# The last 256 rows of a row mean: blocks split over partitions, two-source sums and an indicator matmul

## The chip, the cores and the metric

The kernel runs on one core of one Trainium2 chip. The metric is the device time in microseconds (us) of one execution; lower is better.

## The reference

```python
x = np.random.randn(64, 256, 8192).astype(np.float32)   # 16384 rows of 8192, 537 MB
return np.mean(x, axis=2)                               # 16384 means
```

## The kernel before

63 "pairs" of 256 rows (two rows a partition, 8 MiB, called pair 1 to 63 below) stream through three buffers, and VectorE (called DVE in the profiles) reduces each with one instruction. The last 256 rows are two blocks of 128 rows: the first comes as one load, the last in four column chunks (9/16, 1/4, 1/8 and 1/16 of the row). DVE and ScalarE (ACT) share the sums of the last pair and of these blocks. Declarations and most waits are cut. (In the profiles SPq is the queue on which SyncE issues transfers, PE is TensorE and POOL is GpSimd.)

```python
# SyncE: all loads
for t in range(NP):                                   # NP = 63, NBUF = 3
    if t >= NBUF:
        eng.wait_ge(dve_sem, t - NBUF + 1)            # buffer free again
    eng.dma_start(bufs[t % NBUF][:], x_pair[t]).then_inc(in_sems[t % NBUF], 16)
...
for c in range(NCH):                                  # last 128 rows: 4 column chunks
    sl = slice(offs[c], offs[c] + CH[c])
    eng.dma_start(buf2[:, sl], x_one[T2][:, sl]).then_inc(ch_sems[c], 16)
...
eng.wait_ge(fin_sem, 3)                               # the last store
eng.dma_start(out_q[4 * T2 : 4 * T2 + 4, :], fint[0:P:32, :]).then_inc(out_sems[2], 16)

# VectorE
eng.tensor_reduce(dst, bufs[k][:].rearrange("p (r l) -> p r l", r=R), X, ADD)   # every pair
...
eng.tensor_reduce(part[:, 2:3], buf2[:, offs[3] : offs[3] + CH[3]], X, ADD)     # last chunk
...
eng.tensor_reduce(fin[:, 0:1], part[:, 0:6], X, ADD).then_inc(fin_sem, 1)       # join 6 parts
eng.transpose(fint[:], fin[:]).then_inc(fin_sem, 1)                             # 32x32 blocks
eng.tensor_scalar(fint[:], fint[:], inv, None, mybir.AluOpType.mult).then_inc(fin_sem, 1)

# ScalarE: its share, for example
eng.activation(src, src, Copy, accum_out=dst).then_inc(act_sem, 1)
```

The 32x32 transpose leaves the last 128 results in partitions 0, 32, 64 and 96, 32 in each, so the last store reads four partitions.

## Time and profile before

| what | value | where it is read |
|---|---|---|
| time | 1246.21 us (1245.99 to 1246.72, 3 runs) | timed runs |
| span of the profiled run | 1244.7 us | page |
| one pair to the next, landing to landing | 19.355 us (mean) | landings in the trace |
| landing of pair 63, then the last landing | 1222.02, 1241.64 us | landings in the trace |
| last landing to the issue of the last store | 1.39 us | landing and timeline |
| that issue to the end | 1.69 us | timeline and span |

First the page of the kernel before: busy tenths of DVE and of the DMA engines in 40 equal slices, GB/s in each slice, and the chain of waits.

```profile
DVE  2898988989889889898898988989889898898897
...
DMA  9999999999999999999999999999999999999998
GB/s 436 415 430 438 438 438 438 430 413 438 438 438 438 438 436 411 434 438 438 438 438 438 425 417 438 438 438 438 438 432 411 438 438 438 438 438 436 417 428 373
...
DMA 70%; DVE 29%; issue 0%; SPq 0%; DVEq 0%
...
buf<-in_x_dram SPq DMA_DIRECT2D x63, 40.7
...
buf<-in_x_dram SPq DMA_DIRECT2D x1, 256.0 KB, 20.4
```

The DMA engines are full in all slices but the last: the page gives the packets of the loads' queue 99.8% of the 16 engines' span. A pair is 8,388,608 bytes and one lands every 19.355 us on average, which is 433.4 GB/s. The last number of an issue line is the median time from issue to landing: 40.7 us for a pair, about two periods, so a load always has others queued before it. The chain gives DVE 29% because a load is issued when DVE frees a buffer.

Next the timeline of the end of the kernel before (start, duration, engine, line, operation, operands, and in brackets the idle time and what ended it).

```profile
1202.70 17.22 DVE L121 TENSOR_REDUCE res<-buf 128x2 f32<-128x16384 f32 x1 [2.13 <-DMA buf<-in_x_dram]
...
1222.05 8.69 DVE L133 TENSOR_REDUCE res<-buf 128x1 f32<-128x8192 f32 x1 [2.13 <-DMA buf<-in_x_dram]
...
1231.76 4.42 DVE L135 TENSOR_REDUCE res<-buf 128x1 f32<-128x4096 f32 x1 [1.03 <-DMA buf<-in_x_dram]
...
1237.27 2.42 DVE L137 TENSOR_REDUCE part<-buf 128x1 f32<-128x2176 f32 x1 [1.09 <-DMA buf<-in_x_dram]
...
1241.04 1.06 ACT L159 ACTIVATE buf<-buf 128x1024 f32<-128x1024 f32 x1
1241.66 0.69 DVE L143 TENSOR_REDUCE part<-buf 128x1 f32<-128x512 f32 x1 [0.69 <-DMA buf<-in_x_dram]
...
1242.38 0.16 DVE L149 TENSOR_REDUCE fin<-part 128x1 f32<-128x6 f32 x1
1242.58 0.21 DVE L151 STREAM_TRANSPOSE fint<-fin 128x32 f32<-128x32 f32 x1
1242.82 0.18 DVE L153 TENSOR_SCALAR fint<-fint 128x32 f32<-128x32 f32 x1
1243.03 0.61 SPq L110 DMA_DIRECT2D out_dram<-fint  x1
```

DVE waits for a transfer before each piece. After the last landing come a 0.69 us reduction, the joining of the six parts (three short DVE instructions), and the store. Only the time after 1241.64 us is not covered by the loads: 3.1 us, 0.25% of the span.

### The profile page before, as it was taken

The numbers are of one execution on the slowest core, as the hardware profiler recorded it, in microseconds if no ns is written. First come the engines' busy times: TensorE is split into PE (matmuls) and PEld (weight loads), VectorE is DVE, ScalarE is ACT, GpSimd is POOL, SyncE is SP. The second block draws the span as 40 slices with busy tenths as digits, with TensorE's granted clock in tenths as the row PEclk, the third lists the DMA queues.
The fourth block names the chain that finished last, engine by engine and source line by source line (L and its number), as shares of the span: only waits on it lengthen the run. The fifth ranks groups of instructions, "written<-read, shape, count | busy, mean of one in ns | idle before, by whom it ended". The sixth has DMA issues, their size and how long they took to land.

```text
span 1244.7 us, 315 instructions
## 1 busy us (share of the span) xinstructions
PE 1.7 (0%) x6; PEld 0.6 (0%) x6; DVE 1085.6 (87%) x70; ACT 17.2 (1%) x14; POOL 0.8 (0%) x7
## 2 busy tenths in 40 slices
PE   0000000000000000000000000000000000000000
PEld 0000000000000000000000000000000000000000
DVE  2898988989889889898898988989889898898897
ACT  0000000000000000000000000000000000000005
POOL 0000000000000000000000000000000000000000
DMA  9999999999999999999999999999999999999998
GB/s 436 415 430 438 438 438 438 430 413 438 438 438 438 438 436 411 434 438 438 438 438 438 425 417 438 438 438 438 438 432 411 438 438 438 438 438 436 417 428 373
DMA packets 9874, 536.94 MB, mean 431 GB/s; under 512 B 1106, under 2 KB 1170, under 8 KB 1426
## 3 DMA queue, kind: packets, MB, share of 16 engines
q1 hardware_dynamic: 9874, 536.94, 99.8%
HBM read 536.87 MB, written 0.07 MB: 431 GB/s over the span
## 4 chain that ended last, share of the span: by engine, by line
DMA 70%; DVE 29%; issue 0%; SPq 0%; DVEq 0%
DMA buf<-in_x_dram 70%; DVE res L121 29%; DVEq L121 0%; SPq L101 0%; DVE part L143 0%; SPq L95 0%; DVE fint L151 0%; DVE fint L153 0%; DVE fin L149 0%
## 5 line engine op out<-in xcount | busy, mean ns | idle before, releaser
L121 DVE TENSOR_REDUCE res<-buf 128x16384 f32 (+1 forms) x62 | 1067.6, 17220 | 152.3 <-DMA buf<-in_x_dram 152.3
L159 ACT ACTIVATE buf<-buf 128x1024 f32<-128x1024 f32 (+3 forms) x5 | 15.0, 2994 | 1221.7 <-DMA buf<-in_x_dram 1221.6
L133 DVE TENSOR_REDUCE res<-buf 128x1 f32<-128x8192 f32 x1 | 8.7, 8685 | 2.1 <-DMA buf<-in_x_dram 2.1
L135 DVE TENSOR_REDUCE res<-buf 128x1 f32<-128x4096 f32 x1 | 4.4, 4419 | 1.0 <-DMA buf<-in_x_dram 1.0
L137 DVE TENSOR_REDUCE part<-buf 128x1 f32<-128x2176 f32 x1 | 2.4, 2421 | 1.1 <-DMA buf<-in_x_dram 1.1
L184 PE MATMUL ps<-ident,res 128*63 128x128 f32 x2 | 0.7, 434 | 1230.8 <-DVE res L133 1230.8
L159 ACT ACT_TABLE_LOAD x1 | 1.3, 1283 | 1.8 <-PEq L220 1.8
L143 DVE TENSOR_REDUCE part<-buf 128x1 f32<-128x512 f32 x1 | 0.7, 686 | 0.7 <-DMA buf<-in_x_dram 0.7
L139 DVE TENSOR_REDUCE part<-buf 128x1 f32<-128x1024 f32 x1 | 1.2, 1220 | 0.1
L159 ACT ACTIVATION_READ_ACCUMULATOR buf<-buf 128x1 f32 x5 | 0.9, 186 | 0.0
L184 PEld LDWEIGHTS ps<-ident,res 128*63 128x63 f32 x2 | 0.3, 202 | 1230.8 <-issue 1230.8
L188 PE MATMUL psone<-ident,res 128*1 128x128 f32 x2 | 0.6, 421 | 0.0
L187 PE MATMUL psone<-ident,res 128*1 128x128 f32 x2 | 0.6, 397 | 4.7 <-DVE res L135 4.7
L169 ACT ACTIVATE outsb<-ps 63x128 f32<-63x128 f32 x2 | 0.4, 264 | 0.0
L79 POOL TENSOR_SCALAR_AFFINE_SELECT ident<-ident 128x128 f32<-128x128 f32 x1 | 0.3, 292 | 0.2 <-POOL ident L77 0.2
L171 ACT ACTIVATE out1sb<-psone 1x128 f32<-1x128 f32 x1 | 0.3, 266 | 1.5 <-PE psone L188 1.5
L188 PEld LDWEIGHTS psone<-ident,res 128*1 128x1 f32 x2 | 0.3, 128 | 0.2
L151 DVE STREAM_TRANSPOSE fint<-fin 128x32 f32<-128x32 f32 x1 | 0.2, 212 | 0.0
L153 DVE TENSOR_SCALAR fint<-fint 128x32 f32<-128x32 f32 x1 | 0.2, 181 | 0.0
L77 POOL MEMSET ident<- 128x128 f32 x1 | 0.2, 204 | 0.0
L149 DVE TENSOR_REDUCE fin<-part 128x1 f32<-128x6 f32 x1 | 0.2, 159 | 0.0
L76 POOL MEMSET fin<- 128x32 f32 x1 | 0.1, 125 | 1.3 <-POOLq L220 1.3
(5 smaller groups left out, 0.5 us busy)
## 6 DMA issues: line engine op xcount, KB each, us to landing
buf<-in_x_dram SPq DMA_DIRECT2D x1, 4096.0 KB, 31.1
buf<-in_x_dram SPq DMA_DIRECT2D x1, 2304.0 KB, 17.3
buf<-in_x_dram SPq DMA_DIRECT2D x1, 1024.0 KB, 19.4
buf<-in_x_dram SPq DMA_DIRECT2D x63, 40.7
buf<-in_x_dram SPq DMA_DIRECT2D x1, 512.0 KB, 20.2
buf<-in_x_dram SPq DMA_DIRECT2D x1, 256.0 KB, 20.4
out_dram<-outsb SPq DMA_DIRECT2D x1, 63.0 KB
out_dram<-out1sb SPq DMA_DIRECT2D x1, 0.5 KB
```

Of the source, the lines that this page charges most:

```text
L79: eng.affine_select(out=ident[:], in_=ident[:], compare_op=mybir.AluOpType.not_equal, fill=1.0, base=0, pattern=[[-1, P]], channel_multipl ...
L121: eng.tensor_reduce(dst, bufs[k][:].rearrange("p (r l) -> p r l", r=R), X, ADD).then_inc(dve_sem, 1)
L133: eng.tensor_reduce(res[:, t, 0:1], bufs[t % NBUF][:, :L], X, ADD).then_inc(dve_sem, 1)
L135: eng.tensor_reduce(res1[:, 0:1], buf1[:, : L // 2], X, ADD).then_inc(dve_sem, 1)
L137: eng.tensor_reduce(part[:, 0:1], buf2[:, :s0], X, ADD).then_inc(dve_sem, 1)
L139: eng.tensor_reduce(part[:, 1:2], buf2[:, offs[1] : offs[1] + s1], X, ADD).then_inc(dve_sem, 1)
L143: eng.tensor_reduce(part[:, 2:3], buf2[:, offs[3] : offs[3] + CH[3]], X, ADD).then_inc(dve_sem, 1)
L159: eng.activation(src, src, Copy, accum_out=dst).then_inc(act_sem, 1)
L169: eng.activation(outsb[:, :, r], ps[r][:], Copy, scale=inv).then_inc(cp_sem, 1)
L184: eng.transpose(ps[r][:], res[:, :, r], ident[:]).then_inc(pe_sem, 1)
L187: eng.matmul(psone[:], res1[:, 0:1], ident[:], start=True, stop=False)
L188: eng.matmul(psone[:], res1[:, 1:2], ident[:], start=False, stop=True).then_inc(pe_sem, 1)
```

## The change

The change puts the last 256 rows into blocks of 128, 64, 32 and 32 rows. A block of n rows is spread over all 128 partitions, 128/n parts a row. Each piece is summed by one DVE instruction that adds its two halves element by element and accumulates; ACT no longer sums. TensorE multiplies each column of partial sums with an indicator matrix, which adds up the parts of a row and leaves a block's results as one row in PSUM (the tiles `psb`). The 256 results gather in one row of one partition and go out in one store. The diff, cut to its core:

```diff
-    CH = [9 * L // 16, L // 4, L // 8, L // 16]
+    BLOCKS = [(128, [L]), (64, [L // 2]), (32, [L // 4])]
+    BLOCKS.append((32, [L // 8, 5 * L // 64, 3 * L // 64]))
...
+            src = x_rows[row : row + n].rearrange("r (q l) -> (r q) l", q=P // n)
...
+            eng.tensor_tensor(ind64[:], ident[:, 0:P:2], ident[:, 1:P:2], ADD)   # GpSimd
+            eng.tensor_tensor(ind32[:], ind64[:, 0:64:2], ind64[:, 1:64:2], ADD)
...
-            eng.dma_start(out_q[4 * T2 : 4 * T2 + 4, :], fint[0:P:32, :])
+            eng.dma_start(out_pair[NP : NP + 1, :], lastsb[:])
...
+            def fast(dst, run, scale=1.0):
+                h = run.shape[-1] // 2
+                return eng.tensor_tensor_reduce(
+                    out=run[:, 0:h], in0=run[:, 0:h], in1=run[:, h:],
+                    scale=scale, scalar=0.0, op0=ADD, op1=ADD, accum_out=dst,
+                )
...
+            for i, (k, n, src, place) in enumerate(pieces):
+                eng.wait_ge(ch_sems[i], 16)
+                fast(part[:, i : i + 1], place, inv).then_inc(part_sem, 1)
+            eng.wait_ge(pe_sem, R + NBLK)
+            eng.tensor_copy(lastsb[:, EARLY:], psb[-1][:, :n]).then_inc(last_sem, 1)
...
-            acc(part[:, 5:6], buf2[:, offs[2] : offs[2] + CH[2]])               # ACT's sums
...
+                mm = eng.matmul(
+                    psb[k][:, :n], part[:, i : i + 1], ind[n][:], start=start, stop=stop
+                )
```

The two sums of the last pair use the same `fast`; the other 62 pairs keep their reduction.

More of the change, by code (lines that the diff above doesn't have):

```diff
@@ L27, in bass_global_avg_pool_1d_kernel @@
     NBUF = 3
-    CH = [9 * L // 16, L // 4, L // 8, L // 16]
-    assert sum(CH) == L
-    NCH = len(CH)
+    BLOCKS = [(128, [L]), (64, [L // 2]), (32, [L // 4])]
+    BLOCKS.append((32, [L // 8, 5 * L // 64, 3 * L // 64]))
+    assert sum(n for n, _ in BLOCKS) == R * P
+    assert all(sum(ch) * P == n * L for n, ch in BLOCKS)
+    NBLK = len(BLOCKS)
+    EARLY = sum(n for n, _ in BLOCKS[:-1])
+    NCH = sum(len(ch) for _, ch in BLOCKS)
     x_rows = x.rearrange("b c l -> (b c) l")
     x_pair = x_rows.rearrange("(t p r) l -> t p (r l)", p=P, r=R)
-    x_one = x_rows.rearrange("(t p) l -> t p l", p=P)
-    out_flat = out.rearrange("b c -> (b c)")
-    out_pair = out_flat.rearrange("(t n) -> t n", n=R * P)
-    out_one = out_flat.rearrange("(t p) -> t p", p=P)
-    out_q = out_flat.rearrange("(t q) -> t q", q=32)
-    T1 = R * NP
-    T2 = R * NP + 1
+    out_pair = out.rearrange("b c -> (b c)").rearrange("(t n) -> t n", n=R * P)
     with ExitStack() as ctx:
@@ L45, in bass_global_avg_pool_1d_kernel @@
         res = E(nc.sbuf_tensor("res", [P, NP, R], f32))
-        res1 = E(nc.sbuf_tensor("res1", [P, 2], f32))
-        part = E(nc.sbuf_tensor("part", [P, 8], f32))
-        fin = E(nc.sbuf_tensor("fin", [P, 32], f32))
-        fint = E(nc.sbuf_tensor("fint", [P, 32], f32))
+        part = E(nc.sbuf_tensor("part", [P, NCH], f32))
         ident = E(nc.sbuf_tensor("ident", [P, P], f32))
+        ind64 = E(nc.sbuf_tensor("ind64", [P, 64], f32))
+        ind32 = E(nc.sbuf_tensor("ind32", [P, 32], f32))
+        ind = {128: ident, 64: ind64, 32: ind32}
         outsb = E(nc.sbuf_tensor("outsb", [NP, P, R], f32))
-        out1sb = E(nc.sbuf_tensor("out1sb", [1, P], f32))
+        lastsb = E(nc.sbuf_tensor("lastsb", [1, R * P], f32))
         ps = [E(nc.psum_tensor(f"ps{r}", [NP, P], f32)) for r in range(R)]
-        psone = E(nc.psum_tensor("psone", [1, P], f32))
+        psb = [E(nc.psum_tensor(f"psb{k}", [1, P], f32)) for k in range(NBLK)]
         in_sems = [E(nc.semaphore(f"in_sem{i}")) for i in range(NBUF)]
-        one_sem = E(nc.semaphore("one_sem"))
         ch_sems = [E(nc.semaphore(f"ch_sem{i}")) for i in range(NCH)]
         dve_sem = E(nc.semaphore("dve_sem"))
-        act_sem = E(nc.semaphore("act_sem"))
+        part_sem = E(nc.semaphore("part_sem"))
         prep_sem = E(nc.semaphore("prep_sem"))
@@ L63, in bass_global_avg_pool_1d_kernel @@
         cp_sem = E(nc.semaphore("cp_sem"))
-        fin_sem = E(nc.semaphore("fin_sem"))
-        out_sems = [E(nc.semaphore(f"out_sem{i}")) for i in range(3)]
-        b1 = NP % NBUF
-        b2 = (NP + 1) % NBUF
-        buf1 = bufs[b1]
-        buf2 = bufs[b2]
-        offs = [sum(CH[:i]) for i in range(NCH)]
-        s0 = CH[0] // 2 - L // 64
-        s1 = CH[1] // 2
+        last_sem = E(nc.semaphore("last_sem"))
+        out_sems = [E(nc.semaphore(f"out_sem{i}")) for i in range(2)]
+        pieces = []
+        row, at = NP * R * P, 0
+        for k, (n, ch) in enumerate(BLOCKS):
+            src = x_rows[row : row + n].rearrange("r (q l) -> (r q) l", q=P // n)
+            col = 0
+            for w in ch:
+                place = bufs[(NP + min(k, 1)) % NBUF][:, at + col : at + col + w]
+                pieces.append((k, n, src[:, col : col + w], place))
+                col += w
+            row += n
+            at = at + col if k else 0
         def gpsimd_program(eng):
-            eng.memset(fin[:], 0.0).then_inc(prep_sem, 1)
             eng.memset(ident[:], 0.0).then_inc(prep_sem, 1)
-            eng.wait_ge(prep_sem, 2)
+            eng.wait_ge(prep_sem, 1)
             eng.affine_select(
@@ L87, in gpsimd_program @@
             ).then_inc(prep_sem, 1)
+            eng.wait_ge(prep_sem, 2)
+            eng.tensor_tensor(ind64[:], ident[:, 0:P:2], ident[:, 1:P:2], ADD).then_inc(
+                prep_sem, 1
+            )
+            eng.wait_ge(prep_sem, 3)
+            eng.tensor_tensor(ind32[:], ind64[:, 0:64:2], ind64[:, 1:64:2], ADD).then_inc(
+                prep_sem, 1
+            )
         first = len(nc.main_func.blocks[0].instructions)
@@ L95, in sync_program @@
                 eng.dma_start(bufs[t % NBUF][:], x_pair[t]).then_inc(in_sems[t % NBUF], 16)
-            eng.wait_ge(dve_sem, NP - NBUF + 1)
-            eng.dma_start(buf1[:, :L], x_one[T1]).then_inc(one_sem, 16)
-            eng.wait_ge(dve_sem, NP - NBUF + 2)
-            for c in range(NCH):
-                sl = slice(offs[c], offs[c] + CH[c])
-                eng.dma_start(buf2[:, sl], x_one[T2][:, sl]).then_inc(ch_sems[c], 16)
+            for i, (k, n, src, place) in enumerate(pieces):
+                if i < 2:
+                    eng.wait_ge(dve_sem, NP - NBUF + 1 + i)
+                eng.dma_start(place, src).then_inc(ch_sems[i], 16)
             eng.wait_ge(cp_sem, 2)
@@ L106, in sync_program @@
             )
-            eng.wait_ge(cp_sem, 3)
-            eng.dma_start(out_one[T1 : T1 + 1, :], out1sb[:]).then_inc(out_sems[1], 16)
-            eng.wait_ge(fin_sem, 3)
-            eng.dma_start(out_q[4 * T2 : 4 * T2 + 4, :], fint[0:P:32, :]).then_inc(
-                out_sems[2], 16
-            )
+            eng.wait_ge(cp_sem, R + NBLK - 1)
+            eng.wait_ge(last_sem, 1)
+            eng.dma_start(out_pair[NP : NP + 1, :], lastsb[:]).then_inc(out_sems[1], 16)
             for s in out_sems:
@@ L123, in pair @@
                 ).then_inc(dve_sem, 1)
+            def fast(dst, run, scale=1.0):
+                h = run.shape[-1] // 2
+                return eng.tensor_tensor_reduce(
+                    out=run[:, 0:h],
+                    in0=run[:, 0:h],
+                    in1=run[:, h:],
+                    scale=scale,
+                    scalar=0.0,
+                    op0=ADD,
+                    op1=ADD,
+                    accum_out=dst,
+                )
             trips = (NP - 1) // NBUF
@@ L131, in vector_program @@
             t = NP - 1
-            eng.wait_ge(in_sems[t % NBUF], 16 * (t // NBUF + 1))
-            eng.tensor_reduce(res[:, t, 0:1], bufs[t % NBUF][:, :L], X, ADD).then_inc(dve_sem, 1)
-            eng.wait_ge(one_sem, 16)
-            eng.tensor_reduce(res1[:, 0:1], buf1[:, : L // 2], X, ADD).then_inc(dve_sem, 1)
-            eng.wait_ge(ch_sems[0], 16)
-            eng.tensor_reduce(part[:, 0:1], buf2[:, :s0], X, ADD).then_inc(dve_sem, 1)
-            eng.wait_ge(ch_sems[1], 16)
-            eng.tensor_reduce(
-                part[:, 1:2], buf2[:, offs[1] : offs[1] + s1], X, ADD
-            ).then_inc(dve_sem, 1)
-            eng.wait_ge(ch_sems[3], 16)
-            eng.tensor_reduce(
-                part[:, 2:3], buf2[:, offs[3] : offs[3] + CH[3]], X, ADD
-            ).then_inc(dve_sem, 1)
-            eng.wait_ge(dve_sem, NP + 4)
-            eng.wait_ge(act_sem, 5)
-            eng.wait_ge(prep_sem, 1)
-            eng.tensor_reduce(fin[:, 0:1], part[:, 0:6], X, ADD).then_inc(fin_sem, 1)
-            eng.wait_ge(fin_sem, 1)
-            eng.transpose(fint[:], fin[:]).then_inc(fin_sem, 1)
-            eng.wait_ge(fin_sem, 2)
-            eng.tensor_scalar(
-                fint[:], fint[:], inv, None, mybir.AluOpType.mult
-            ).then_inc(fin_sem, 1)
-        def scalar_program(eng):
-            def acc(dst, src):
-                eng.activation(src, src, Copy, accum_out=dst).then_inc(act_sem, 1)
-            t = NP - 1
-            eng.wait_ge(in_sems[t % NBUF], 16 * (t // NBUF + 1))
-            acc(res[:, t, 1:2], bufs[t % NBUF][:, L:])
-            eng.wait_ge(one_sem, 16)
-            acc(res1[:, 1:2], buf1[:, L // 2 : L])
+            for r in range(R):
+                if r == 0:
+                    eng.wait_ge(in_sems[t % NBUF], 16 * (t // NBUF + 1))
+                fast(res[:, t, r : r + 1], bufs[t % NBUF][:, r * L : (r + 1) * L]).then_inc(
+                    dve_sem, 1
+                )
+            for i, (k, n, src, place) in enumerate(pieces):
+                eng.wait_ge(ch_sems[i], 16)
+                fast(part[:, i : i + 1], place, inv).then_inc(part_sem, 1)
+            eng.wait_ge(pe_sem, R + NBLK)
+            n = BLOCKS[-1][0]
+            eng.tensor_copy(lastsb[:, EARLY:], psb[-1][:, :n]).then_inc(last_sem, 1)
+        def scalar_program(eng):
             for r in range(R):
@@ L169, in scalar_program @@
                 eng.activation(outsb[:, :, r], ps[r][:], Copy, scale=inv).then_inc(cp_sem, 1)
-            eng.wait_ge(pe_sem, 3)
-            eng.activation(out1sb[:], psone[:], Copy, scale=inv).then_inc(cp_sem, 1)
-            eng.wait_ge(ch_sems[0], 16)
-            acc(part[:, 3:4], buf2[:, s0 : CH[0]])
-            eng.wait_ge(ch_sems[1], 16)
-            acc(part[:, 4:5], buf2[:, offs[1] + s1 : offs[1] + CH[1]])
-            eng.wait_ge(ch_sems[2], 16)
-            acc(part[:, 5:6], buf2[:, offs[2] : offs[2] + CH[2]])
+            at = 0
+            for k, (n, _) in enumerate(BLOCKS[:-1]):
+                eng.wait_ge(pe_sem, R + 1 + k)
+                eng.activation(lastsb[:, at : at + n], psb[k][:, :n], Copy).then_inc(cp_sem, 1)
+                at += n
         def tensor_program(eng):
-            eng.wait_ge(prep_sem, 3)
-            eng.wait_ge(dve_sem, NP)
-            eng.wait_ge(act_sem, 1)
+            eng.wait_ge(prep_sem, 4)
+            eng.wait_ge(dve_sem, NP + 1)
             for r in range(R):
                 eng.transpose(ps[r][:], res[:, :, r], ident[:]).then_inc(pe_sem, 1)
-            eng.wait_ge(dve_sem, NP + 1)
-            eng.wait_ge(act_sem, 2)
-            eng.matmul(psone[:], res1[:, 0:1], ident[:], start=True, stop=False)
-            eng.matmul(psone[:], res1[:, 1:2], ident[:], start=False, stop=True).then_inc(pe_sem, 1)
+            for i, (k, n, src, place) in enumerate(pieces):
+                start = i == 0 or pieces[i - 1][0] != k
+                stop = i == NCH - 1 or pieces[i + 1][0] != k
+                eng.wait_ge(part_sem, i + 1)
+                mm = eng.matmul(
+                    psb[k][:, :n], part[:, i : i + 1], ind[n][:], start=start, stop=stop
+                )
+                if stop:
+                    mm.then_inc(pe_sem, 1)
         sync_program(nc.sync)
```

## The prediction

> **What bounds the kernel now.** The page's DMA row reads 9 in every slice but the last and the mean is 431 GB/s: the kernel streams 537 MB and the transfers set the pace. DVE is 87% busy but in the timeline each 17.22 us pair reduction is followed by about 2.1 us of waiting for a transfer. Two loads are always queued (issue to landing 40.7 us, one lands every 19.35 us), so DVE and ACT work before the last landing does not count. The time is: first landing 22.1 us, the stream until 1241.66 us (start of the last chunk's reduction), and a tail. The tail by the timeline: chunk reduction 0.69, final reduction, 32x32 transpose and scaling until 1243.0 (1.37 us from landing to the output's issue), then 1.65 us for the output store, 0.61 of it on the issuing queue. Only those 3 us, 0.25% of the span, can shrink.
>
> **What changes.**
> 1. Sums. ACT's share (five activations, 15.0 us) goes; DVE sums the two halves of each run with a two-source instruction. Estimate [...]with the 1.04 ns an element of the reduction (17.22 us for 16384)[...]: 4.5 us for a 128x8192 row set (8.69 as a reduction), 2.4, 1.3, 0.8, 0.6 and 0.45 us for the later pieces. [...]this trace has no such instruction, so the rate is the chief unknown.
> 2. Transfers. Same 8 MB in the last 256 rows, in six loads instead of five, all on 128 partitions. From the trace's 2.42 us per MiB, landings fall at about 1231.7, 1236.6, 1239.0, 1240.3, 1241.1 and 1241.65. I expect at most 0.2 us for the extra load and small packets.
> 3. DVE schedule at that rate: two sums of the last pair 1222.05 to 1231.0, then each piece starts nearly at its landing; the last sum ends near 1242.15. DVE just keeps up.
> 4. Tail. Last sum 0.45, one fp32 indicator matmul about 0.5 (the 128-column one took 0.59 in two passes), PSUM copy 0.2, hand-offs 0.1: about 1.3 us against 1.37. A draw.
> 5. Store. One row of 1 KB from one partition instead of four pieces of 128 bytes; the one-partition store of before took 0.25 us to issue, the four-partition one 0.61: perhaps 0.3 us saved.
> 6. GpSimd's indicator sums run at the start, off the path.
>
> **Critical path.** DVE time saved in the last 20 us was hidden behind transfers. Expected change: -0.3 us, within the run-to-run spread (1245.99 to 1246.72).
>
> **Predicted** 1245.9 us, 8 in 10 within 1244.9 to 1247.4. Faster by over 2%: 0.003; within 2%: 0.985; slower: 0.012.
>
> **What would show it.** Groups: the 128x8192 two-source sum at 4.3 to 4.7 us. DMA view: still about 431 GB/s; last landing within 0.3 us of 1241.66. Timeline: DVE waiting for a transfer before the last pieces, not the reverse; 1.2 to 1.5 us from last landing to output issue; output issue 0.25 to 0.4 us.
>
> **What would make it wrong.** If the two-source sum takes two cycles a pair, each 8192 costs 8.7 us on one engine where ACT used to help: DVE falls behind by about 15 us, so about 1261 us.[...]

The forecast came to 1245.9 us: 1246.2 us before, less 0.3 for the store, with the rest of the tail a draw. Terms that no trace of this case showed are cut and marked: in step 1 the rate supposed for the two-source sum, its source, and a fixed time for each sum, which was a guess; in the last paragraph a sentence on what else a custom instruction could cost. The times of step 1, 4.5 us for the 4096 pairs of a 128x8192 row set and so on, follow if a pair takes the 1.04 ns that the reduction takes for an element (from 0.69 us for 512 elements and 8.69 us for 8192 in the trace before), with the fixed time on top; the trace after shows 1.042 ns a pair and 0.16 us fixed. A "cycle" in the last paragraph stands for those 1.04 ns, and its 8.7 us are the 8.69 us of the measured reduction. The 0.2 us for the extra load in step 2, and the copy and hand-offs in step 4, are estimates; measured are +0.07 us from pair 63 to the last landing, 0.18 us for the copy, and 0.04 to 0.08 us for each hand-off in the timeline after. The "two passes" of step 4 are the two MATMUL records that the trace has for one matmul of the kernel, 0.59 us together.

## The result and the profile after

The changed kernel takes 1245.33 us (median, 1245.10 to 1245.54, 4 runs) against 1246.31 us for the kernel before (1245.99 to 1246.72, 4 runs of the same rounds). The ratio is 0.9992, with a 95% interval of 0.9975 to 1.0009. A ratio here is the mean time of one kernel's fast runs over that of the other's of the same rounds, so it is not quite the ratio of the medians quoted. The interval alone does not prove a gain. The traces, in which the last 3 us repeat within 0.01 to 0.07 us (below), show one.

The page of the changed kernel, the same rows as before:

```profile
DVE  2898988989889888898898988989889898898988
...
DMA  9999999999999999999999999999999999999998
GB/s 436 415 430 438 438 438 426 417 438 438 438 438 438 436 407 438 438 438 438 438 434 409 438 438 438 438 438 434 409 438 438 438 438 438 432 411 438 438 438 373
...
DMA 70%; DVE 29%; issue 0%; SPq 0%; DVEq 0%; PE 0%
...
buf<-in_x_dram SPq DMA_DIRECT2D x63, 40.7
...
buf<-in_x_dram SPq DMA_DIRECT2D x1, 192.0 KB, 20.0
```

Nothing moved in the stream: the same 40.7 us from issue to landing, the same full slices. The timeline of the changed kernel's end (the two-source sum stands there as CUSTOM_DVE_ANT_0, with a DVE_READ_ACCUMULATOR2_ANT of 0.08 us at its end that writes the sum):

```profile
1222.13 4.43 DVE L137 CUSTOM_DVE_ANT_0 buf<-buf 128x4096 f32<-128x4096 f32 x1 [2.13 <-DMA buf<-in_x_dram]
...
1231.84 4.43 DVE L137 CUSTOM_DVE_ANT_0 buf<-buf 128x4096 f32<-128x4096 f32 x1 [0.94 <-DMA buf<-in_x_dram]
...
1236.73 2.29 DVE L137 CUSTOM_DVE_ANT_0 buf<-buf 128x2048 f32<-128x2048 f32 x1 [0.46 <-DMA buf<-in_x_dram]
...
1239.23 1.23 DVE L137 CUSTOM_DVE_ANT_0 buf<-buf 128x1024 f32<-128x1024 f32 x1 [0.20 <-DMA buf<-in_x_dram]
...
1240.51 0.69 DVE L137 CUSTOM_DVE_ANT_0 buf<-buf 128x512 f32<-128x512 f32 x1
...
1241.34 0.49 DVE L137 CUSTOM_DVE_ANT_0 buf<-buf 128x320 f32<-128x320 f32 x1
...
1241.81 0.36 DVE L137 CUSTOM_DVE_ANT_0 buf<-buf 128x192 f32<-128x192 f32 x1
...
1241.89 0.61 PE L188 MATMUL psb<-ind,part 128*1 128x32 f32 x4 [0.36 <-DVE part L137]
1242.10 0.08 DVE L137 DVE_READ_ACCUMULATOR2_ANT part<- 128x1 f32 x1
...
1242.54 0.18 DVE L166 COPY lastsb<-psb 1x32 f32<-1x32 f32 x1 [0.36 <-PE psb L188]
1242.80 0.25 SPq L121 DMA_DIRECT2D out_dram<-lastsb  x1
```

The DVE waits get shorter from piece to piece: 0.94, 0.46 and 0.20 us, then no gap worth a bracket. The last sum starts at 1241.81 us and its data landed at 1241.79. So DVE just keeps pace with the transfers: it comes free within 0.05 us of the last landing.

The groups of the changed kernel, kept apart by form, give the rate of the new sum (busy us, mean ns of one):

```profile
L137 DVE CUSTOM_DVE_ANT_0 buf<-buf 128x4096 f32<-128x4096 f32 x3 | 13.2, 4425 | 3.1 <-DMA buf<-in_x_dram 3.1
...
L137 DVE CUSTOM_DVE_ANT_0 buf<-buf 128x192 f32<-128x192 f32 x1 | 0.4, 357 | 0.0
```

From 192 to 4096 pairs of elements it takes 4425 - 357 = 4068 ns more, 1.042 ns a pair. The reduction takes 17,220 ns for 16,384 elements, 1.05 ns an element. In the time of one element of the reduction the two-source sum takes in two.

The difference of 0.78 us between the two spans, as a ledger (landings and starts as read from the traces, in us):

| step | before | after | difference |
|---|---|---|---|
| landing of pair 63 | 1222.02 | 1222.10 | +0.08 |
| from there to the last landing | 19.61 | 19.69 | +0.07 |
| last landing to issue of the last store | 1.39 | 1.02 | -0.38 |
| that issue to the end | 1.69 | 1.14 | -0.55 |
| span | 1244.73 | 1243.95 | -0.78 |

The first line is jitter: in the twelve traces whose pair loop is not unrolled, pair 63 lands between 1221.67 and 1222.38 us. The last two lines repeat within 0.01 us in every trace of a kernel with the same end, the second within 0.07 us, so the last two can be attributed. Of the 0.38 us, 0.32 lie in the last sum: it ended 0.71 us after the last landing and now ends 0.39 us after it. The join from there to the issue took 0.68 us and takes 0.63.

### The profile page after: what moved, and what is told of

It reads as the page before. It is cut to its first block, busy times and chain, and to the rows that moved or that the text cites. A ratio compares the mean times of both kernels' runs of the same rounds, so it can differ in the third digit from the quotient of the medians.

```text
span 1243.9 us, 331 instructions
## 1 busy us (share of the span) xinstructions
PE 2.7 (0%) x14; PEld 0.8 (0%) x14; DVE 1086.1 (87%) x79; ACT 2.4 (0%) x6; POOL 1.2 (0%) x8
## 4 chain that ended last, share of the span: by engine, by line
DMA 70%; DVE 29%; issue 0%; SPq 0%; DVEq 0%; PE 0%
DMA buf<-in_x_dram 70%; DVE res L130 29%; DVEq L130 0%; SPq L113 0%; DVE buf L137 0%; SPq L109 0%; PE psb L188 0%; DVE lastsb L166 0%; DVE part L137 0%
## 5 line engine op out<-in xcount | busy, mean ns | idle before, releaser
L130 DVE TENSOR_REDUCE res<-buf 128x16384 f32 (+1 forms) x62 | 1067.6, 17220 | 152.4 <-DMA buf<-in_x_dram 152.4
L137 DVE CUSTOM_DVE_ANT_0 buf<-buf 128x4096 f32<-128x4096 f32 (+5 forms) x8 | 18.2, 2292 | 3.9 <-DMA buf<-in_x_dram 3.7
## 6 DMA issues: line engine op xcount, KB each, us to landing
buf<-in_x_dram SPq DMA_DIRECT2D x63, 40.7
```

Of the source, the lines that this page charges most:

```text
L137: return eng.tensor_tensor_reduce(out=run[:, 0:h], in0=run[:, 0:h], in1=run[:, h:], scale=scale, scalar=0.0, op0=ADD, op1=ADD, accum_out=dst,)
```

## The experiments

My theory was that transfers set the pace and that the gain lies wholly after the last landing, 0.55 us in the store and 0.38 us in the last sum and join. The rivals were that it is noise, that the shorter DVE sums as such bring it, as DVE's 29% of the chain suggests, or that the split of rows helps the reads.

### a_again: the changed kernel, timed again

> The changed kernel unedited, timed in five rounds, to learn whether the difference is real. Theory (ledger of the two traces): last landing +0.15 us, landing to output issue -0.38 us, output issue to end -0.55 us, so 0.8 us faster, a ratio near 0.9994 and an interval that leaves 1 out. Rival (noise): the ratio's interval holds 1 and the medians of the rounds overlap.

No edit. 1245.63 us (1245.33 to 1245.83, 5 runs) against 1246.19 us (1245.74 to 1246.79, 9 runs of the kernel before). Ratio 0.9994, interval 0.9981 to 1.0008. The ratio is as expected, but against the expectation the interval holds 1, and the two ranges overlap, so the times alone leave the rival standing. The trace does not: 1.02 us from landing to issue and 1.14 us from issue to end, as in the first trace of this kernel.

### b_store1 and b_store4: what makes the last store shorter

> Before, with the last store cut to one partition and 128 bytes (96 results wrong on purpose). Theory: the store from four partitions costs the 0.55 us; from issue to end falls from 1.70 to about 1.15 us, its issue from 0.61 to 0.25 us, and the time by 0.5 to 0.6 us; all else unchanged. Rival (the gain comes from the sums or the blocks, or from the size of the pieces): the time from issue to end stays near 1.7 us and the time falls by less than 0.2 us.

```diff
-eng.dma_start(out_q[4 * T2 : 4 * T2 + 4, :], fint[0:P:32, :])
+eng.dma_start(out_q[4 * T2 : 4 * T2 + 1, :], fint[0:1, :])
```

> Before, with the last store still of four partitions of 128 bytes, but the adjacent partitions 0 to 3 instead of 0, 32, 64 and 96 (96 results wrong on purpose). Theory 1 (the number of partitions counts): from issue to end stays 1.65 to 1.75 us, its issue about 0.6 us. Theory 2 (the stride of 32 partitions counts): issue about 0.25 us and 1.15 us from issue to end, as with one partition.

```diff
-eng.dma_start(out_q[4 * T2 : 4 * T2 + 4, :], fint[0:P:32, :])
+eng.dma_start(out_q[4 * T2 : 4 * T2 + 4, :], fint[0:4, :])
```

Both give wrong results for 96 rows on purpose. The store of b_store1, then of b_store4, in their timelines:

```profile
1242.98 0.23 SPq L110 DMA_DIRECT2D out_dram<-fint  x1
```

```profile
1243.28 0.25 SPq L110 DMA_DIRECT2D out_dram<-fint  x1
```

With one partition the issue takes 0.23 us and the end comes 1.10 us after it; with four adjacent partitions 0.25 and 1.18 us; with partitions 0, 32, 64 and 96, in the kernel before, 0.61 and 1.69 us. b_store1 took 1245.59 us (1245.41 to 1246.21) against 1246.19 us, ratio 0.9996 (0.9983 to 1.0010); b_store4 was one look (1246.19 us, state unknown, so no verdict from its time). The 0.55 us are in the store, as the theory said. But the number of partitions is hardly the reason: theory 2 of b_store4 holds, on its one trace. Four packets of 128 bytes leave in all the four-partition cases, so it is the place of the four partitions (a stride of 32 instead of 1) that costs, 0.36 us on the issuing queue and 0.15 us after it. Why a strided source costs that is not settled here.

### b_join: only the join replaced

> Before, with only the join replaced: final reduction kept, then a matmul with the identity and a scaled PSUM copy in place of the 32x32 transpose, and one row stored from one partition. Theory: landing to output issue grows from 1.39 to 1.6 to 1.75 us (a two-pass matmul of 128 columns, about 0.55 us, and 0.2 us for the copy, against 0.45 us for transpose and scaling), the store shrinks by 0.55 us: 0.2 to 0.4 us faster in all. Rival (the join itself is what gains): 0.7 us faster or more.

```diff
-eng.transpose(fint[:], fin[:])
-eng.tensor_scalar(fint[:], fint[:], inv, None, mult)
+eng.matmul(psfin[:], fin[:, 0:1], ident[:], start=True, stop=True)      # TensorE
+eng.tensor_scalar(out2sb[:], psfin[:], inv, None, mult)                 # DVE, from PSUM
-eng.dma_start(out_q[4 * T2 : 4 * T2 + 4, :], fint[0:P:32, :])
+eng.dma_start(out_one[T2 : T2 + 1, :], out2sb[:])
```

Correct. Landing to issue 1.96 us, above the range I gave (1.6 to 1.75): from the end of the final reduction until DVE starts its copy 0.74 us pass for a matmul of 128 columns, and that copy takes 0.28 us. Issue to end 1.12 us. So the join costs 0.57 us more and the store gives 0.57 us back, and the time is 1246.17 us (1245.60 to 1246.20) against 1246.19 us: the 0.2 to 0.4 us that I expected did not come. The rival, that the matmul join is itself the gain, falls.

### b_two: only DVE's sums made two-source

> Before, with only DVE's sums of the last 384 rows made two-source (ACT keeps its share). Theory: only the last 512-column sum counts, 0.69 us becomes about 0.50 us to the end of the accumulator read; but ACT's last sum ends at 0.56 us after the last landing and then binds, so 0.1 to 0.2 us faster. Rival (shorter DVE sums as such bring the gain): 0.7 us faster or more, as the change as a whole.

The edit replaces the five `tensor_reduce` of DVE in the last pair, the block and the chunks by the `fast` of the change; ACT keeps its share. Landing to issue falls from 1.39 to 1.28 us, store 1.70 us as before. The last DVE sum ends 0.45 us after the last landing, but the final reduction, which waits for ACT too, starts at 0.63 us; ACT's last accumulator read ends at 0.54 us:

```profile
1241.66 0.19 ACT L162 ACTIVATION_READ_ACCUMULATOR buf<-buf 128x1 f32 x1
...
1241.94 0.16 DVE L152 TENSOR_REDUCE fin<-part 128x1 f32<-128x6 f32 x1 [0.17 <-DVE part L127]
```

That fits the expectation that ACT binds (the bracket names DVE, but DVE's sum had ended 0.09 us before ACT's). So the two-source sum of the old last chunk ends 0.26 us earlier than the reduction did (0.45 instead of 0.71 us after the landing), but while ACT still sums, only 0.11 us of that reach the store. The rest, from 0.45 to 0.39 us, is left for the smaller last piece of the changed kernel; no run changes that alone. Time 1245.70 us (1245.58 to 1246.52), ratio 0.9999 (0.9985 to 1.0012); the time cannot resolve 0.11 us. Halving DVE's sums while ACT still helps gains a tenth of a microsecond, not the 0.9 of the whole change.

### a_nosplit: the last 128 rows not split over partitions

> The changed kernel with the last 128 rows on 128 partitions in column pieces (half, quarter, eighth, 5/64, 3/64 of the row), the same bytes a load, and an identity matmul of 128 columns, instead of blocks of 64, 32 and 32 rows. Theory: sums and landings as in the changed kernel; the last matmul writes 128 columns and is seen 0.3 to 0.45 us later, the PSUM copy takes 0.28 instead of 0.18 us (as seen when before got that join): landing to output issue 1.35 to 1.6 us instead of 1.02, store unchanged at 1.14 us, so 0.4 to 0.5 us slower than the changed kernel. Rival (splitting rows helps through contiguous reads): the last landing comes 0.3 us later or more as well.

```diff
-BLOCKS = [(128, [L]), (64, [L // 2]), (32, [L // 4])]
-BLOCKS.append((32, [L // 8, 5 * L // 64, 3 * L // 64]))
+BLOCKS = [(128, [L])]
+BLOCKS.append((128, [L // 2, L // 4, L // 8, 5 * L // 64, 3 * L // 64]))
```

The end of its timeline:

```profile
1241.47 0.36 DVE L137 CUSTOM_DVE_ANT_0 buf<-buf 128x192 f32<-128x192 f32 x1
...
1242.61 0.28 DVE L166 COPY lastsb<-psb 1x128 f32<-1x128 f32 x1 [0.77 <-PE psb L188]
1242.98 0.25 SPq L121 DMA_DIRECT2D out_dram<-lastsb  x1
```

The copy waits 0.77 us for the matmul (0.36 in the changed kernel) and takes 0.28 us (0.18). Landing to issue 1.53 us, within the range expected; from pair 63 to the last landing 19.68 us, as in the changed kernel (19.69), so contiguous reads of the split blocks bring nothing that can be seen. Time 1245.85 us (1245.66 to 1246.43), 0.36 us over a_relief, a little under the 0.4 to 0.5 us expected. With three matmuls back to back on PE before that copy (six MATMUL records in one run of 1.63 us), part of the 0.77 us could have been queueing; but b_join, with one such matmul alone, shows 0.74. What the split buys is a narrow last join: 32 columns instead of 128.

### a_relief and a_extra: how much slack DVE has in the last 20 us

> The changed kernel with the second half of the last pair (128 x 8192) summed by ACT again, as before the change, so DVE has 4.4 us less to do before the last blocks. Theory: the last piece's sum already starts within 0.05 us of its landing, so nothing is gained: landing to output issue stays at 1.02 us within 0.1, DVE only waits longer for the transfers, time within 0.2 us of the changed kernel (ratio to before 0.9994). Rival (DVE's load in the last 20 us still costs time after the change): landing to issue falls by 0.2 us or more.

```diff
-fast(res[:, t, r : r + 1], bufs[t % NBUF][:, r * L : (r + 1) * L])    # r = 0 and 1
+fast(res[:, t, 0:1], bufs[t % NBUF][:, :L])                           # DVE
+eng.activation(half, half, Copy, accum_out=res[:, t, 1:2])            # ACT; half = bufs[t % NBUF][:, L:]
```

Correct, landing to issue 1.02 us, time 1245.49 us (1245.18 to 1245.76), ratio 0.9992 (0.9978 to 1.0005) against 1246.38 us. DVE waits 5.28 us before the next block instead of 0.94 and nothing is gained: less DVE work than in the changed kernel is worth nothing.

> The changed kernel with one more DVE reduction (128 x 4096, result unused, 4.4 us) after the two sums of the last pair. Theory: DVE waits only 0.94 + 0.46 + 0.20 us for transfers after that point, so all but these 1.6 us come out at the end: the last sum starts 2.8 us after its landing and the time is 2.6 to 3.0 us longer. Rival (DVE work before the last landing is hidden, as the prediction says): no change, within 0.3 us.

```diff
+eng.tensor_reduce(junk[:], bufs[t % NBUF][:, L // 2 : L], X, ADD)     # after the last pair's sums
```

Correct. The timeline of a_extra, DVE only:

```profile
1235.26 4.41 DVE L138 CUSTOM_DVE_ANT_0 buf<-buf 128x4096 f32<-128x4096 f32 x1
...
1239.60 2.28 DVE L138 CUSTOM_DVE_ANT_0 buf<-buf 128x2048 f32<-128x2048 f32 x1
...
1243.99 0.35 DVE L138 CUSTOM_DVE_ANT_0 buf<-buf 128x192 f32<-128x192 f32 x1
```

No bracket is left: DVE never waits again, and the last sum starts at 1243.99 us although its data landed at 1241.89. Landing to issue 3.08 us, 2.07 more than in the changed kernel; time 1247.68 us (1247.44 to 1247.86), 2.2 us over a_relief. More DVE work does come out at the end, against the rival, but less than the 2.6 to 3.0 I expected. I had counted three waits (1.60 us). The small gaps between the last sums vanish too (0.05 and 0.13 us in the timeline after), and sums that follow each other without a wait start while the accumulator read of the one before, 0.08 us, still runs.

### a_reduce: the two-source sums taken away

> The changed kernel with every two-source sum put back to a one-source reduction on DVE (the scaling moved to the PSUM copies); ACT does not come back. Theory: 8.69 us each for the three 128 x 8192 sums, then 4.42, 2.3, 1.22, 0.83 and 0.55 us, with no wait after 1222.1: the last sum ends near 1257.5 instead of 1242.2, so 15.3 us slower, near 1260.8 us. Rival (DVE work before the last landing is hidden): within 1 us of the changed kernel.

```diff
-return eng.tensor_tensor_reduce(out=run[:, 0:h], in0=run[:, 0:h], in1=run[:, h:], ...)
+return eng.tensor_reduce(dst, run, X, ADD)
```

The timeline of a_reduce from pair 63 on, DVE and the last store:

```profile
1222.41 17.28 DVE L136 TENSOR_REDUCE res<-buf 128x1 f32<-128x8192 f32 x2 [2.13 <-DMA buf<-in_x_dram]
1239.60 17.51 DVE L136 TENSOR_REDUCE part<-buf 128x1 f32<-128x8192 f32 x6
...
1257.47 0.18 DVE L156 TENSOR_SCALAR lastsb<-psb 1x32 f32<-1x32 f32 x1 [0.36 <-PE psb L178]
1257.74 0.25 SPq L121 DMA_DIRECT2D out_dram<-lastsb  x1
```

Correct, 1259.87 us (1259.44 to 1260.22, 4 runs) against 1246.24 us, ratio 1.0109 (1.0093 to 1.0124). Landing to issue is 15.70 us, 14.7 more; I expected 15.3, again because sums that follow each other overlap a little (the six of the last blocks take 17.92 us one by one, 17.51 together). This is the only experiment whose interval is clear of 1. It also shows what the two-source sum is for: it does not make the kernel faster, it pays for ACT's absence.

### a_steady, a_loop and a_unroll: the two-source sum for every pair

> The changed kernel with the two-source sum for every pair, not only the last one: DVE per pair 2 x 4.4 = 8.9 us instead of 17.2, loop unrolled. Theory (the stream of transfers sets the pace): DVE busy falls from 87% to about 45%, the buffers come free 8.4 us earlier, the loads queue longer (about 49 us from issue to landing instead of 40.7) and the time does not change, within 0.5 us. In the chain of waits DVE's share falls from 29% to about 15% and DMA's rises by the same. Rival (DVE's 29% of the chain is time that can be saved): 14% of the span, about 170 us, is saved.

```diff
-with eng.Fori(0, trips) as i: ...                  # one tensor_reduce a pair
+for t in range(NP - 1):                            # unrolled
+    eng.wait_ge(in_sems[t % NBUF], 16 * (t // NBUF + 1))
+    fast(res[:, t, 0:1], bufs[t % NBUF][:, :L])
+    fast(res[:, t, 1:2], bufs[t % NBUF][:, L:]).then_inc(dve_sem, 1)
```

Correct, 1246.84 us (1246.67 to 1247.04, 4 runs) against 1246.38 us, ratio 1.0002 (0.9987 to 1.0018). The rival's 170 us are nowhere. But it is also 1.35 us over a_relief, outside the 0.5 us of my theory. The page of a_steady:

```profile
PE 2.7 (0%) x14; PEld 0.8 (0%) x14; DVE 562.7 (45%) x265; ACT 2.4 (0%) x6; POOL 1.2 (0%) x8
...
q14 instruction: 2, 0.02, 0.0%
...
DMA 77%; DVE 18%; another core or an unknown queue 5%; SPq 0%; issue 0%; PE 0%
```

A queue that the changed kernel's page does not list has appeared: two packets of instructions. In the landings of a_steady, two pairs come 20.27 and 20.32 us after the one before; all others 19.34 to 19.37. At each of the two places the trace has one 8 KB packet of 0.32 us on one DMA engine, and the 64 KB packet that starts just as it ends took 3.08 us instead of 2.42. A pair has landed when the slowest of 16 full engines is done: of the first late pair 15 parts land by 254.02 us and the last at 254.94. The delay stays to the end: pair 63 lands at 1223.49 us, more than 1 us after the latest of the twelve traces above. The next two runs test that.

> The two-source sum for every pair again, but in the loop that the changed kernel has instead of 62 unrolled pairs. Theory: the 1.5 us that the unrolled version lost come from its two instruction fetches in mid-stream (8 KB each; the two landings next to them came 20.3 us apart instead of 19.35). In the loop there are none, every landing comes 19.35 us after the one before, and the time is the changed kernel's within 0.3 us, although DVE is busy 45% instead of 87%. Rival (two-source sums beside the stream slow the transfers): the time stays 1 us or more above the changed kernel's.

The edit is the same sum inside the `Fori` loop that the changed kernel has. Correct, 1245.40 us (1245.00 to 1245.49, 5 runs) against 1246.24 us, ratio 0.9993 (0.9979 to 1.0007). The page of a_loop:

```profile
PE 2.7 (0%) x14; PEld 0.8 (0%) x14; DVE 562.7 (45%) x265; ACT 2.4 (0%) x6; POOL 1.2 (0%) x8
...
q1 hardware_dynamic: 10010, 536.94, 99.9%
...
DMA 84%; DVE 8%; issue 7%; SPq 0%; DVEq 0%; PE 0%
```

No instruction queue, pair 63 at 1222.05 us, and the changed kernel's time, with DVE busy 45% instead of 87%. In the chain the DVE share halves (8% plus 7% of "issue", which in this chain is time inside the first sum of each pair) and DMA's share grows from 70% to 84%: the time saved on DVE turns into time that a load waits in the queue (49.1 us from issue to landing instead of 40.7).

> The changed kernel with its pair loop unrolled and nothing else (one-source reductions as in the changed kernel). Theory: about half as many extra instructions on DVE as in the unrolled two-source version, so one instruction fetch in mid-stream, one landing about 20.3 us after the one before, and 0.9 to 1.0 us more time. Rival (unrolling is not the cause): no such landing and the changed kernel's time within 0.3 us.

The edit unrolls the changed kernel's own loop, with its reduction. Correct, 1246.01 us (1245.80 to 1246.35, 4 runs), 0.61 us over a_loop, ratio to before 0.9998 (0.9983 to 1.0013). The page has one instruction packet,

```profile
q14 instruction: 1, 0.01, 0.0%
```

the trace has it in mid-stream, and one pair lands 20.10 us after the one before, so 0.75 us late. One fetch as expected, its cost somewhat below the 0.9 to 1.0 us expected. Unrolling is the cause, not the two-source sum: between 200 and 1220 us, the fourteen traces have only three 64 KB packets of over 2.6 us, and each of the three starts as an instruction packet ends.

No experiment beats the changed kernel: a_loop and a_relief equal it.

## Why the prediction was right

The prediction of 1245.9 us (1244.9 to 1247.4) held; 1245.33 us was measured. Point by point:

- **What bounds the kernel.** Right. With DVE's work on the pairs halved (a_loop) the time does not move.
- **Step 1, the sum's rate.** Right: 4.43 us against 4.5 predicted for a 128x8192 row set, and 2.29, 1.23, 0.69, 0.49 and 0.36 us for the later pieces. The fixed part was a guess; what is left beside 1.042 ns a pair is 0.16 us. That a pair would take what an element of the reduction takes (1.05 ns) was the estimate; no trace had shown it before the change ran.
- **Steps 2 and 3, landings and schedule.** Right: predicted 1231.7, 1236.6, 1239.0, 1240.3, 1241.1 and 1241.65 us, measured 1231.82, 1236.71, 1239.21, 1240.49, 1241.31 and 1241.79; the last sum ends at 1242.18 against 1242.15.
- **Step 4, "A draw".** Mis-sized. I gave 1.3 us from the last landing to the output's issue; it is 1.02, so 0.38 us are gained. The last sum ends 0.39 us after the landing instead of 0.45, and the matmul term was the largest error: from the end of the sum to the start of the copy 0.36 us pass, hand-off included, where I had put 0.5 for the matmul alone, from a matmul of 128 columns. With 128 columns (a_nosplit) the same wait is 0.77 us, and the whole stretch 1.53. So it was not a draw.
- **Step 5, the store.** The direction was right, the size (0.3) and the reason were not. It saves 0.55 us: 0.36 in the issue, as I had read, and 0.19 after it. I ascribed it to one partition instead of four; b_store4 shows that four adjacent partitions are nearly as quick.
- **"DVE and ACT work before the last landing does not count."** True of the kernel before, but too broad. It holds while DVE still waits for the last pieces. In the changed kernel that margin is 1.6 us of visible waits: 4.4 us more work cost 2.1 us (a_extra), 14.7 us came back without the two-source sum (a_reduce). The prediction's own warning, about 1261 us if a 128x8192 sum takes 8.7 us, is that case; a_reduce gives 1259.9.

The errors of steps 4 and 5 add up to 0.56 us in the same direction (0.31 and 0.25), and the measured time lies 0.57 us below the point predicted. That these agree so closely is partly luck, since the runs of one kernel spread by 0.4 us and more. The range of 2.5 us also holds the time before and three times the gain forecast, so the hit says little of the change; the steps, read in the traces, do.

Open: why a source with a stride of 32 partitions makes a small store slower; the jitter of 0.7 us in the stream (in the twelve traces most of it arises by the ninth pair, up to 0.76 us in sum against at most 0.21 us after that); and whether the 0.56 and 0.98 us between the medians would hold in an interval with more runs. The traces show 0.93 us less after the last landing in both traces of the changed kernel; the intervals of its times hold 1.

## What to carry to other kernels

When transfers fill the span, cost a change by what happens after the last landing and take that from the timeline, landing by landing; a share in the chain of waits that comes from freeing buffers is no saving (a_loop: DVE's work halved, time unchanged). Work before the last landing is free only up to the waits that the engine still has, and these can be added up beforehand, though only roughly (a_extra: 2.6 to 3.0 us expected, 2.1 measured). The last store belongs to that stretch: where its source lies cost 0.5 us here, more than the new sum and join gained. Unrolling the pair loop gained nothing here: the landings next to instruction packets in mid-stream came 0.92 and 0.97 us (a_steady) and 0.75 us (a_unroll) late, and the unrolled kernels took 1.4 us (medians, on two chips) and 0.6 us more than a_loop.
